# A third of the position bias made at the start of the kernel, its comparisons on GpSimd

## The chip, the cores and the metric

The kernel runs on one NeuronCore of one Trainium2 chip. The metric is the device time of one execution in microseconds (us), taken as the median of several runs. The engines are TensorE (PE in the profile; its weight loads stand apart as PEld), VectorE (DVE), ScalarE (ACT), GpSimd (POOL) and SyncE (SP), which here does nothing but issue transfers. Each engine works through its own queue in order; semaphores tie the queues together.

## The reference

A decoder trunk of two layers on 256 tokens of width 1024. Each layer is a half-step feed-forward network (FFN), an attention, and a second FFN half-step, each behind an RMS norm whose shift, scale and gate come from a conditioning vector `c`. The attention of the first layer adds a learned bias that depends on the bucket of the distance between two positions and on the head. Cut to what matters here:

```python
D_MODEL, SEQ, D_FF, MOBA_HEADS, REL_BUCKETS = 1024, 256, 2816, 16, 32

def swiglu(h, w_gate, w_up, w_down):
    return (jax.nn.silu(h @ w_gate) * (h @ w_up)) @ w_down
...
    c_act = jax.nn.silu(c)
    for layer in range(DEPTH):
        mods = c_act @ ada_w[layer] + ada_b[layer]
        sh1, sc1, g1, sh2, sc2, g2, sh3, sc3, g3 = jnp.split(mods, 9, axis=-1)
        h = modulate(rms_norm(x, norm_g[layer, 0]), sh1, sc1)
        x = x + 0.5 * g1[:, None, :] * swiglu(h, ffn_w_gate[layer, 0], ffn_w_up[layer, 0], ffn_w_down[layer, 0])
        ...
# inside the first layer's attention
        bias = bias_t[h5, t5_bucket(qp[:, None, :, None, None] - kpos)]
        s = jnp.einsum("bhqd,bhqnkd->bhqnk", qc, kg).astype(jnp.float32) * scale + bias.astype(jnp.float32)
        mask = (kidx <= qi[None, None, :, None, None]) & sv[None, None, :, :, None]
        s = jnp.where(mask, s, NEG)
```

## The kernel before, in words

All weights are float32 and are read once from HBM, 264 MB in all. A product of two float32 matrices is made on TensorE as three products of a rounded part ("hi") and the rest ("lo"): ScalarE makes hi from the raw tile (line 699 for the weights of most of the kernel), VectorE makes lo as raw minus hi (line 700), and the result is hi·hi + hi·lo + lo·hi. The conditioning vectors are not made on TensorE: VectorE multiplies tiles of `ada_w` with the broadcast of silu(`c`), called `c_b`, and sums (line 713, "a column dot" below).

**The start** is the function `first`. It makes the first 768 of the 2816 columns of gate and up of the first FFN while their weights and the first shift and scale come in, in eight chunks k = 0 to 7 of 128 rows of the input. Before chunk 0: silu(`c`) and its hi and lo (lines 1762 to 1764), eight small matmuls that broadcast it into PSUM (1768), two copies into `c_b` (1771), the sum of squares of the two halves of the tokens x0 and x1 (1789 on VectorE, 1786 on ScalarE), their root on GpSimd (`rstd`, line 889), two diagonal matrices of it (`diag`, 1793), and the scaled transposes of x (1803 for k = 0 and 1, 1808 after). Then for each chunk: two column dots (713) and one small scaling (717), `z` (1820), hi and lo of the input `h` (867, 868), hi and lo of the weights (`whi` 1831, `wlo` 1832), and 36 matmuls into six accumulators (1840 to 1842). TensorE multiplies zeros (1779, 1810) where it would have nothing to do.

**The bias** is the generator `bias_steps`. It is cut into 12 blocks: 4 groups c of 32 keys for each of three pairs of a query half t and a key half kb. For 8 comparison rows i of a group one comparison each, "query position at least key position plus bucket edge", gives a matrix of 0 and 1 in bf16 (`oh`): the even i on VectorE (line 1417, `is_ge`), the odd ones on ScalarE (1415, `Sign`, which gives -1 and 1 and so has its own table of halves). For kb = 0 it covers both query halves, 128x256. A block is then 24 matmuls (line 1396) of `oh` with three bf16 parts of the table of bucket steps (`tab`), a copy out of PSUM into `bt` (1403 on VectorE, which adds the causal mask where t equals kb, 1405 on ScalarE otherwise), and a store to `bias_d` in HBM (1406), from where the attention reads it back (1451). What comes before is `own`, `least`, `key`, `below`, `blk`, `rows` and the six parts of `tab`: small VectorE instructions (1365 to 1389), and 32 memsets of `low` on GpSimd (1359). The generator is stepped in the FFN after the start, among the matmuls of lines 1081 and 1087; `hold` keeps all of it behind a modelled time of 40 us (`HELD`).

**The order** of the work is not that of the code. The class `Order` takes all instructions with what they depend on, places them on the engines by a table of durations, and writes the order down for each engine; `ranked` gives an instruction a rank that puts it early, `hold` a time before which it isn't placed. It then tries disturbed orders, one for each seed of the list `TRIALS`, and keeps the best by its own table. The rank and the seeds so decide each queue, and the queue decides what waits behind what.

**The buffers** that the change touches: `ps_mm` has four PSUM banks (`mm_tile`), `ps_tr` four (`tr_tile`); `modp` has two SBUF tiles of 128x1024 called `gate`, first used for a gate vector at 144 us.

Of the kernel before, what the change touches and what calls it, by code (L numbers as in the profile page):

```python
# [31 lines left out]
B1 = 6  # L32
# [30 lines left out]
EARLY = 2  # L63
SIDE_TO = 6
# [129 lines left out]
def bcast_row(ap, n, parts=P):  # L194
# [21 lines left out]
TRIALS = (200001, 200002, 200017, 200027, 200038, 200039, 200043, 200053, 200064, 200109, 200195, 200238, 200274,  # L216
          200368, 200395, 200459, 200494, 200524, 200550, 200577, 200753, 200848, 200852, 200862, 200928, 201042,
          201579, 201676, 202214, 202513, 202702, 202901, 203186, 203712, 204111, 204899, 207186)
# [377 lines left out]
def trunk(ctx: ExitStack, tc: tile.TileContext, a: dict, out: bass.AP):  # L596
# [742 lines left out]
    groups = []  # L1339

    def bias_steps():
# [6 lines left out]
        with ExitStack() as st:  # L1348
            bp = st.enter_context(tc.tile_pool(name="bp", bufs=1))
            posi = bp.tile([P, S], I32, name="posi")  # L1350
            nc.sync.dma_start(posi, bcast_row(pos_f, S))
            btab = bp.tile([P, 3 * H + NT * NB], F32, name="btab")
            nc.sync.dma_start(btab, a["tab"])
            tab, prev, end = [btab[:, i * H:(i + 1) * H] for i in range(3)]
            keyi = btab[:, 3 * H:].bitcast(I32).rearrange("p (t b) -> p t b", t=NT)
            yield
# [3 lines left out]
            yield  # L1360
# [3 lines left out]
            posq = bp.tile([P, S], F32, name="posq")  # L1364
# [7 lines left out]
            yield  # L1372
# [3 lines left out]
            def parts():  # L1376
                blk = bp.tile([P, 4], F32, name="blk")
                V.tensor_reduce(blk, ident.rearrange("p (j b) -> p j b", b=NB), axis=AX.X, op=ALU.add)
                V.tensor_tensor(tab, prev, tab, op=ALU.subtract)
                for signs in range(2):  # L1380
                    rows = bp.tile([P, 4, H], F32, tag="rows", name=nm("rows"))
                    if signs:
                        V.tensor_tensor(tab, tab, end, op=ALU.subtract)
                    V.scalar_tensor_tensor(rows, blk[:, :, None].to_broadcast([P, 4, H]), 0.5 if signs else 1.0,
                                           tab[:, None, :].to_broadcast([P, 4, H]), op0=ALU.mult, op1=ALU.mult)
                    for i in range(3):
                        V.tensor_copy(pieces[signs][i], rows)
                        if i < 2:
                            V.tensor_tensor(rows, rows, pieces[signs][i], op=ALU.subtract)
            groups.append(parts)  # L1390

            def mms(kb, t, c, oh):
                pt = tr_tile()
# [499 lines left out]
```

## Time and profile before

| | |
|---|---|
| median of 3 runs | 974.61 us (974.39 to 976.02) |
| the profiled execution | 975.75 us, its span 974.0 us |
| TensorE, weight loads, VectorE, ScalarE, GpSimd busy | 99%, 85%, 89%, 64%, 7% |
| granted clock of TensorE | 1.00 |
| read from HBM, mean rate | 258.5 MB, 270 GB/s |

The span runs from the first to the last instruction of the profiled execution; its own time is 1.75 us more. In the timeline a row begins with the start in us from the span's start and the duration in us, then engine, line, operation, output and inputs, shape and count; what stands in square brackets is idle time of the engine before the row and what ended it. Rows of like instructions in a row are merged (x and a count). A matmul's duration covers its way through a pipelined array, so the distance between the starts of two neighbours, and not the duration, is what one costs.

### The profile page before, as it was taken

What the parts mean: (1) busy time and instruction counts of PE and PEld (TensorE: products, weight loads), DVE (VectorE), ACT (ScalarE), POOL (GpSimd) and SP (SyncE); (2) the same over time, 40 slices, a digit from 0 to 9 for tenths busy, and PEclk for the clock granted to TensorE, in tenths of its full rate; (3) what the DMA queues carried; (4) which work ended last, traced back from release to release, by engine and by line L of the source; (5) the groups of instructions that cost most, each with busy time, mean ns of one, the idle gap of its engine ahead of it and who ended that gap; (6) DMA issues with size and microseconds to landing.
All of it is one profiled execution on the core that took longest, in us unless ns stands there. A gap on an engine that the chain in (4) does not pass through costs nothing.

```text
span 974.0 us, 15262 instructions
## 1 busy us (share of the span) xinstructions
PE 962.7 (99%) x5516; PEld 823.7 (85%) x5516; DVE 871.2 (89%) x1587; ACT 618.6 (64%) x1158; POOL 70.0 (7%) x112
## 2 busy tenths in 40 slices
PE   8999999999999999999999999999999999999998
PEld 6988888888888788888888888888888888888887
DVE  7999899799999999999789999986899889768998
ACT  5697565378757965665367655553769886566561
POOL 1000000012230100000000000000143010000000
PEclk9999999999999999999999999999999999999999
DMA  9968789888886688888978798994533476544542
GB/s 368 409 226 298 293 315 360 319 306 332 285 319 225 236 310 344 324 341 312 362 299 320 289 344 339 353 351 172 171 110 116 150 278 254 192 173 175 198 180 81
DMA packets 54283, 263.73 MB, mean 271 GB/s; under 512 B 6304, under 2 KB 7104, under 8 KB 35904
## 3 DMA queue, kind: packets, MB, share of 16 engines
q1 hardware_dynamic: 51840, 255.93, 70.1%
q0 software_dynamic: 1888, 6.32, 2.1%
q8 instruction: 43, 0.70, 0.3%
q10 hardware_dynamic: 480, 0.51, 0.2%
q14 instruction: 32, 0.26, 0.1%
HBM read 258.52 MB, written 4.22 MB: 270 GB/s over the span
## 4 chain that ended last, share of the span: by engine, by line
PE 86%; DVE 5%; DMA 5%; issue 1%; ACT 1%; POOL 0%; SPq 0%; ACTq 0%; DVEq 0%
PE mm L1081 23%; PE mm L852 14%; PE mm L854 14%; PE mm L853 14%; PE mm L1087 12%; DMA raw<-in_first_dram 3%; DVE lo L700 2%; PE at L1294 1%; PE at L1237 1%; PE at L1274 1%; PE tr L902 1%; DMA raw<-in_w_dram 1%; PE mm L1634 1%; DMA bias_d<-bt 1%; PE tr L1670 1%
## 5 line engine op out<-in xcount | busy, mean ns | idle before, releaser
L699 ACT ACTIVATE hi<-raw 128x1024 fp32r<-128x1024 f32 (+1 forms) x308 | 312.5, 1035 | 148.4 <-PE mm L854 81.9
L700 DVE TENSOR_TENSOR lo<-raw,hi 128x1024 fp32r<-128x1024 f32 (+1 forms) x308 | 359.8, 1194 | 31.7 <-ACT hi L699 31.2
L1081 PE MATMUL mm<-h,hi 128*128 128x512 f32 x1120 | 263.5, 391 | 0.9 <-DVE g L1001 0.9
L1081 PEld LDWEIGHTS mm<-h,hi 128*128 128x128 f32 x1120 | 207.7, 188 | 42.7 <-DVE g L1001 1.3
L713 DVE CUSTOM_DVE_ANT_0 adaw<-adaw,c_b,cols 128x1024 f32<-128x1024 f32 x160 | 201.4, 1278 | 4.8 <-DMA adaw<-in_ada_dram 2.5
L1087 PEld LDWEIGHTS mm<-h,lo 128*128 128x128 f32 x1120 | 139.4, 192 | 2.7
L1087 PE MATMUL mm<-h,lo 128*128 128x256 f32 x1120 | 141.2, 283 | 0.0
L854 PE MATMUL mm<-hi,gl 128*128 128x512 f32 (+1 forms) x322 | 124.9, 388 | 0.0
L853 PE MATMUL mm<-lo,gh 128*128 128x512 f32 (+1 forms) x322 | 124.9, 388 | 0.0
L852 PE MATMUL mm<-hi,gh 128*128 128x512 f32 (+1 forms) x322 | 124.7, 389 | 0.0
L852 PE MATMUL mm<-hi,h 128*128 128x512 f32 (+1 forms) x240 | 94.2, 398 | 0.0
L853 PE MATMUL mm<-lo,h 128*128 128x512 f32 (+1 forms) x240 | 93.0, 391 | 0.0
L854 PE MATMUL mm<-hi,h 128*128 128x512 f32 (+1 forms) x240 | 91.8, 390 | 0.0
L854 PEld LDWEIGHTS mm<-hi,gl 128*128 128x128 f32 x322 | 60.5, 188 | 12.4
L853 PEld LDWEIGHTS mm<-lo,gh 128*128 128x128 f32 x322 | 60.5, 188 | 12.2
L852 PEld LDWEIGHTS mm<-hi,gh 128*128 128x128 f32 x322 | 60.5, 188 | 12.2 <-DVE u L1001 0.2
L1000 ACT ACTIVATE g<-mm 128x256 f32<-128x256 f32 x70 | 26.6, 380 | 57.2 <-PE mm L1087 57.0
L852 PEld LDWEIGHTS mm<-hi,h 128*128 128x128 f32 x240 | 45.1, 188 | 9.3 <-issue 1.3
L854 PEld LDWEIGHTS mm<-hi,h 128*128 128x128 f32 x240 | 45.1, 188 | 8.8 <-issue 0.2
L853 PEld LDWEIGHTS mm<-lo,h 128*128 128x128 f32 x240 | 45.0, 188 | 7.8
L1001 DVE TENSOR_TENSOR g<-mm,g 128x256 f32<-128x256 f32 x70 | 29.5, 421 | 20.4 <-ACT g L1000 19.2
L1331 POOL TENSOR_TENSOR hr<-hv,mhalf 128x4 f32<-128x4 f32 (+1 forms) x24 | 37.4, 1562 | 64.7 <-DVE hv L1330 59.5
(260 smaller groups left out, 1230.9 us busy)
## 6 DMA issues: line engine op xcount, KB each, us to landing
raw<-in_w_dram SPq DMA_DIRECT2D x143, 1024.0 KB, 5.5
adaw<-in_ada_dram SPq DMA_DIRECT2D x160, 512.0 KB, 6.0
raw<-in_w_dram SPq DMA_DIRECT2D x10, 512.0 KB, 4.8
raw<-in_first_dram SPq DMA_DIRECT2D x7, 512.0 KB, 9.0
bias_d<-bt SPq DMA_DIRECT2D x12, 256.0 KB, 4.4
gate<-gate_d POOLq DMA_DIRECT2D x6, 512.0 KB, 6.7
bg<-bias_d POOLq DMA_DIRECT2D x4, 768.0 KB, 5.9
raw<-in_first_dram SPq DMA_DIRECT2D x10, 256.0 KB, 8.9
```

The source lines that it names most:

```text
L699: nc.scalar.activation(hi, src, AF.Copy)
L700: nc.vector.tensor_tensor(lo, src, hi.bitcast(F32), op=ALU.subtract)
L713: nc.vector.tensor_tensor_reduce(wt, wt, c_b, 1.0, start, op0=ALU.mult, op1=ALU.add, accum_out=col)
L852: nc.tensor.matmul(ps, lh, rh, start=start, stop=False)
L853: nc.tensor.matmul(ps, lh, rl, start=False, stop=False)
L854: nc.tensor.matmul(ps, ll, rh, start=False, stop=stop)
L902: nc.tensor.transpose(kslice(pt, j), kslice(y, j), ident)
L1000: nc.scalar.activation(x, ps[:, S:], AF.Copy)
L1001: nc.vector.tensor_tensor(x, ps[:, :S], x, op=ALU.add)
L1081: nc.tensor.matmul(ps, wh, both, start=k == 0, stop=False)
L1087: nc.tensor.matmul(ps, wl, hh, start=False, stop=stop)
L1331: nc.gpsimd.tensor_tensor(r, v2, mhalf[:, :nh], op=ALU.pow)
```

## The change

Four of the 12 blocks, those of key half 0 with c = 0 and 1, are made in `first`, ahead of chunk 0. The positions, the table, `key`, the first three parts of `tab` and the comparisons come to the front. Of the 16 comparisons of 128x256, 14 are GpSimd's (`BY_POOL`: all i but 6) and 2 are VectorE's; all use `is_ge`. The mask is added by a matmul of the identity with the bf16 mask, not by VectorE. The four blocks accumulate in the four banks of `ps_mm`, are copied by ScalarE (`FORE_COPY`) into the two `gate` tiles, and are stored from there, not before a modelled time of 48 us (`FORE_OUT`). Four of the six accumulators of the first weights now take over those banks, two take `ps_tr`. The transfer of `cols` moves from ScalarE's queue to GpSimd's. After `first` the pool of the gate tiles `gh` and `gl` is opened anew. The seeds are others, so the order may differ anywhere.

On GpSimd the queue begins, after five constants, like this before; `ssq` is the sum of squares of a half of the tokens, `inv` a table for later, `low` the bucket edges:

```order
masks.py:197 MEMSET ident 128x128
masks.py:199 ISA
masks.py:199 AFFINE_SELECT ident<-ident 128x128
L674 MEMSET mask 128x256
L675 AFFINE_SELECT mask<-mask 128x256
L889 TENSOR_TENSOR rstd_215<-ssq_38_212,mhalf 128x1
L889 TENSOR_TENSOR rstd_222<-ssq_41_218,mhalf 128x1
L1531 MEMSET inv 128x1 x16
L1359 MEMSET low 128x1 x32
```

Now the same place reads, from the two casts of the identity and the mask on; `oh_180` are the comparisons of c = 0, `oh_181` those of c = 1:

```order
L1411 CAST mask_b<-mask 128x128
L1410 CAST ident_b<-ident 128x128
L1400 TENSOR_SCALAR oh_180<-posi,key 128x256 x5
L896 TENSOR_TENSOR rstd_418<-ssq_47_415,mhalf 128x1
L1400 TENSOR_SCALAR oh_181<-posi,key 128x256 x2
L896 TENSOR_TENSOR rstd_425<-ssq_50_421,mhalf 128x1
L1400 TENSOR_SCALAR oh_181<-posi,key 128x256 x2
L1400 TENSOR_SCALAR oh_180<-posi,key 128x256 x2
L1400 TENSOR_SCALAR oh_181<-posi,key 128x256 x3
L1568 MEMSET inv 128x1 x16
```

The root of the first half stands behind five comparisons, that of the second behind seven, and seven more follow; the transfer of `cols`, the 32 memsets and the two casts stand ahead of them all.

On TensorE the first matmuls of chunk 0 (line 1840, into the accumulators mm and tr) stand in the order before right behind the last scaled transpose:

```order
L1810 LDWEIGHTS zeros
L1810 MATMUL tr_190<-zeros 128x128
L1803 MATMUL tr_189<-diag_221,x_100 128x128
L1840 MATMUL mm_193<-h_106,whi_258 128x256
L1840 MATMUL mm_194<-h_106,whi_258 128x256
L1840 MATMUL mm_192<-h_106,whi_258 128x256
L1840 MATMUL tr_195<-h_106,whi_258 128x256
```

In the order now they stand behind the last of the 96 products of the four blocks (line 1405, into mm_282 to mm_284):

```order
L1405 MATMUL mm_284<-tab_161,oh_181 128x64
L1405 LDWEIGHTS oh_181
L1405 MATMUL mm_284<-tab_162,oh_181 128x64
L1851 LDWEIGHTS zeros
L1851 MATMUL tr_280<-zeros 128x128
...
L1881 MATMUL tr_403<-h_106,whi_461 128x256
L1882 MATMUL tr_403<-h_106,whi_461 128x256
L1881 MATMUL tr_404<-h_106,whi_461 128x256
L1849 MATMUL tr_279<-ident,y_455 128x128
```

All 96 products came ahead of chunk 0, so chunk 0 can't begin before the last comparison is done.

On VectorE the work between the lo part of silu(`c`) and the first column dot was one sum of squares (here "ISA", like the dots):

```order
L1764 TENSOR_TENSOR c_117<-c_115,c_116 32x256
L1789 ISA raw_144,ssq_38_212<-x_99 128x1024
L1789 ISA ssq_38_212 128x1
L713 ISA adaw_126,m_cols<-adaw_126,c_b,cols 128x1024
L713 ISA m_cols 128x1
```

It is now, from the same sum of squares on (its head, from `key` to the first part of `tab`, is left out here):

```order
L1830 ISA raw_234,ssq_47_415<-x_99 128x1024
L1830 ISA ssq_47_415 128x1
L1394 TENSOR_TENSOR rows_172<-rows_172,tab_160 128x64
L1392 CAST tab_161<-rows_172 128x64
L1394 TENSOR_TENSOR rows_172<-rows_172,tab_161 128x64
L1392 CAST tab_162<-rows_172 128x64
L1400 TENSOR_SCALAR oh_180<-posi,key 128x256
L1400 TENSOR_SCALAR oh_181<-posi,key 128x256
L720 ISA adaw_215,m_cols<-adaw_215,c_b,cols 128x1024
```

The rest of the table and two comparisons moved in between the sum of squares and the first column dot.

The diff, cut to its core:

```diff
+FORE = 2
+BY_POOL = (0, 1, 2, 3, 4, 5, 7)
+FORE_OUT = 48e3
+FORE_RANK = 6.5
+FORE_COPY = (lambda nc, o, i: nc.scalar.activation(o, i, AF.Copy), lambda nc, o, i: nc.scalar.activation(o, i, AF.Copy))
...
-TRIALS = (200001, 200002, 200017, ...
+TRIALS = (100002, 100006, 100008, ...
...
             if start:
                 start(units)
+                gq = st.enter_context(tc.tile_pool(name=nm("gp"), bufs=1))
...
-            bp = st.enter_context(tc.tile_pool(name="bp", bufs=1))
+            bp = st.enter_context(tc.tile_pool(name="bp", bufs=1, side="right"))
...
+            def onehot(kb, m, to, how):
+                if how == "sign":
+                    nc.scalar.activation(to, posq[:, kb * P:], AF.Sign, bias=below[:, kb, m:m + 1])
+                else:
+                    how.tensor_scalar(to, posq[:, kb * P:], key[:, kb, m:m + 1], None, op0=ALU.is_ge)
...
+            ident_b, mask_b = [bp.tile([P, P], BF16, name=n) for n in ("ident_b", "mask_b")]
+            nc.gpsimd.tensor_copy(ident_b, ident)
+            nc.gpsimd.tensor_copy(mask_b, mask[:, P:])
+            parts(0)
+            ohs = [bp.tile([P, 8, S], BF16, tag="oh", name=nm("oh"), bufs=2) for _ in range(FORE)]
+            for c, oh in enumerate(ohs):
+                for i in range(8):
+                    onehot(0, 8 * c + i, oh[:, i], nc.gpsimd if i in BY_POOL else V)
+
+            def fore(c, t, pt):
+                home = fore_home[c][:, t * 512:(t + 1) * 512]
+                if t == 0:
+                    ahead_of = mask_b[:, NB * c:NB * (c + 1)]
+                    nc.tensor.matmul(pt, ident_b, ahead_of[:, :, None].to_broadcast([P, NB, H]), start=True, stop=False)
+                products(0, t, ohs[c], pt, False, t > 0)
+                bt, pv = home.rearrange("p (h k) -> p h k", h=H), pt.rearrange("p (m h) -> p h m", h=H)
+                with ranked(FORE_RANK):
+                    FORE_COPY[t](nc, bt, pv)
+                hold(lambda: nc.sync.dma_start(bias_d[t, c], home), FORE_OUT)
...
             for kb in range(NT):
                 n = P * (NT - kb)
-                for c in range(4):
-                    oh = bp.tile([P, 8, n], BF16, tag="oh", name=nm("oh"), bufs=3)
+                for c in range(0 if kb else FORE, 4):
+                    oh = bp.tile([P, 8, n], BF16, tag="oh", name=nm("oh"), bufs=2)
...
         with ExitStack() as st:
+            next(side[0])
             fp = st.enter_context(tc.tile_pool(name="fp", bufs=1))
...
-                nc.scalar.dma_start(all_cols, a["cols"])
+                nc.gpsimd.dma_start(all_cols, a["cols"])
...
-            accs = [tr_tile() if f >= 4 else mm_tile() for f in range(B1)]
-            for f in range(B1):
-                for i in range(4 if 1 <= f < 4 else 1):
-                    nc.tensor.matmul(accs[f], zeros, zeros[:, None].to_broadcast([P, 4, P]), start=i == 0, stop=False)
+            fore = [mm_tile() for _ in fore_groups]
+            for ps in fore[:3]:
+                for i in range(4):
+                    nc.tensor.matmul(ps, zeros, zeros[:, None].to_broadcast([P, 4, P]), start=i == 0, stop=i == 3)
+            for ps, fn in zip(fore, fore_groups):
+                fn(ps)
+            accs = [tr_tile() if f < 2 else mm_tile() for f in range(B1)]
+            for ps in accs:
+                nc.tensor.matmul(ps, zeros, zeros[:, None].to_broadcast([P, 4, P]), start=True, stop=False)
```

More of the change, by code (lines that the diff above doesn't have):

```diff
@@ L1371, in bias_steps @@
             V.tensor_scalar(below, key, -1.0, 0.5, op0=ALU.mult, op1=ALU.add)
-            yield
-            pieces = [[bp.tile([P, 4, H], BF16, name=f"tab{i}{j}") for j in range(3)] for i in range(2)]
[L1376 to L1389, printed above, removed]
@@ L1390, in bias_steps, with parts @@
-            groups.append(parts)
+            pieces = [[bp.tile([P, 4, H], BF16, name=f"tab{i}{j}") for j in range(3)] for i in range(2)]
+            blk = bp.tile([P, 4], F32, name="blk")
+            V.tensor_reduce(blk, ident.rearrange("p (j b) -> p j b", b=NB), axis=AX.X, op=ALU.add)
+            def parts(signs):
+                rows = bp.tile([P, 4, H], F32, tag="rows", name=nm("rows"))
+                V.tensor_tensor(tab, tab if signs else prev, end if signs else tab, op=ALU.subtract)
+                V.scalar_tensor_tensor(rows, blk[:, :, None].to_broadcast([P, 4, H]), 0.5 if signs else 1.0,
+                                       tab[:, None, :].to_broadcast([P, 4, H]), op0=ALU.mult, op1=ALU.mult)
+                for i in range(3):
+                    V.tensor_copy(pieces[signs][i], rows)
+                    if i < 2:
+                        V.tensor_tensor(rows, rows, pieces[signs][i], op=ALU.subtract)
@@ new lines, in onehot, with products @@
+            def onehot(kb, m, to, how):
[3 more added lines that the diff above has]
+                    how.tensor_scalar(to, posq[:, kb * P:], key[:, kb, m:m + 1], None, op0=ALU.is_ge)
+            def products(kb, t, oh, pt, signs, first=True):
+                for i in range(8):
+                    for pi in range(3):
+                        nc.tensor.matmul(pt[:, i * 64:(i + 1) * 64], oh[:, i, (t - kb) * P:(t - kb + 1) * P],
+                                         pieces[i % 2 if signs else 0][pi], start=first and pi == 0,
+                                         stop=pi == 2 and (first or i == 7))
@@ L1392, in mms @@
+            fore_home = [modp.tile([P, D], F32, tag="gate", name=nm("fore")) for _ in range(FORE)]
+            for c in range(FORE):
+                for t in range(NT):
+                    fore_groups.append(lambda pt, c=c, t=t: fore(c, t, pt))
+            yield
+            parts(1)
             def mms(kb, t, c, oh):
                 pt = tr_tile()
-                for i in range(8):
-                    for pi in range(3):
-                        nc.tensor.matmul(pt[:, i * 64:(i + 1) * 64],
-                             oh[:, i, (t - kb) * P:(t - kb + 1) * P], pieces[i % 2][pi], start=pi == 0, stop=pi == 2)
+                products(kb, t, oh, pt, True)
```

23 lines of the change are left out of this document (9 added, 14 removed), and 4 rows, old and new, of the table TRIALS.

## The prediction

> **What bounds the kernel now.** I read the page's busy shares and its chain of waits first, then busy times of four stages (columns: PE, PEld, DVE, ACT, POOL busy in us, granted clock, DMA share, GB/s), then the timeline of the first stage.
>
> ```profile
> span 974.0 us, 15262 instructions
> PE 962.7 (99%) x5516; PEld 823.7 (85%) x5516; DVE 871.2 (89%) x1587; ACT 618.6 (64%) x1158; POOL 70.0 (7%) x112
> PE 86%; DVE 5%; DMA 5%; issue 1%; ACT 1%; POOL 0%; SPq 0%; ACTq 0%; DVEq 0%
> 0.00:12.18 12.18, 8.48 (x42) 4.70 (x42) 6.73 (x18) 7.97 (x17) 3.02 (x26) 1.00 0.86 332
> 12.18:30.00 17.82, 16.74 (x137) 16.33 (x138) 16.48 (x29) 9.54 (x17) 0.00 (x0) 1.00 1.03 405
> 30.00:50.30 20.30, 20.15 (x166) 19.48 (x165) 20.12 (x39) 14.55 (x25) 0.00 (x0) 1.00 1.03 410
> 50.30:116.00 65.70, 65.70 (x610) 57.55 (x609) 60.57 (x142) 50.08 (x104) 1.12 (x32) 1.00 0.73 261
> ```
>
> From 50 us on TensorE is the bound: a product taken off its queue there is worth its own length. From 12.18 to 50.3 us, the eight chunks, three things are close to full at once: transfers (share 1.03), VectorE (idle 1.34 + 0.18 = 1.5 us) and TensorE. Before 12.18 us TensorE has nothing to multiply but zeros, and GpSimd hardly works.
>
> ```profile
> 0.99 5.31 PE L1779 MATMUL mm<-zeros 128*128 128x512 bf16 x13 [0.99 <-DVE zeros L1724]
> 4.83 1.21 DVE L1789 CUSTOM_DVE_ANT_0 raw<-x 128x1024 f32<-128x1024 f32 x1
> 6.13 0.57 POOL L889 TENSOR_TENSOR rstd<-ssq,mhalf 128x1 f32<-128x1 f32 x1 [4.09 <-DVE ssq L1789]
> 8.24 0.69 ACT L1793 ACTIVATE diag<-ident,rstd 128x128 f32<-128x128 f32 x2
> 8.39 1.28 DVE L713 CUSTOM_DVE_ANT_0 adaw<-adaw,c_b,cols 128x1024 f32<-128x1024 f32 x1 [2.34 <-ACT c_b L1771]
> 9.23 1.32 ACT L1831 ACTIVATE whi<-raw 128x512 fp32r<-128x512 f32 x2 [0.30 <-DMA raw<-in_first_dram]
> 11.13 0.55 ACT L1820 ACTIVATE z<-tr,m_cols 128x256 f32<-128x256 f32 x1
> 12.16 0.43 DVE L868 TENSOR_TENSOR h<-z,h 128x256 fp32r<-128x256 f32 x1
> 12.18 0.62 PE L1840 MATMUL mm<-h,whi 128*128 128x256 f32 x3 [1.43 <-ACT h L867]
> 49.30 0.28 PE L1842 MATMUL tr<-h,wlo 128*128 128x256 f32 x1
> 50.25 0.28 PE L1842 MATMUL tr<-h,wlo 128*128 128x256 f32 x1
> ACT whi L1831 <- DMA raw<-in_first_dram: 12.6, 8, 2.7
> DVE adaw L713 <- DMA adaw<-in_ada_dram: 1.1, 1, 1.1
> ```
>
> The chunks start when `h` is there (12.18). The last two L1842 rows bracket eight starts: 0.95 / 8 = 0.119 us per matmul. 288 of them and 12 transposes at about the same make 35.7 us of the 38.2 between 12.18 and the end, so TensorE can start 2.5 us later and lose nothing. ScalarE waits 12.6 us for raw weights and has room; VectorE waits 1.1 for a transfer and has almost none.
>
> **What leaves the stage after 50 us.** Four of 12 blocks, 96 of 288 products.
>
> ```profile
> L1396 PE MATMUL tr<-tab,oh 128*128 128x64 bf16 x288 | 11.0, 194 | 0.0
> 70.21 0.84 PE L1396 MATMUL tr<-tab,oh 128*128 128x64 bf16 x23
> 71.21 0.87 PE L1396 MATMUL tr<-tab,oh 128*128 128x64 bf16 x24
> 50.53 7.30 PE mm L1081 x32
> L1417 DVE TENSOR_SCALAR oh<-posq,key 128x256 bf16<-128x256 f32 (+1 forms) x32 | 8.7, 311 | 0.0
> L1387 DVE CAST tab<-rows 128x64 bf16<-128x64 f32 x6 | 1.2, 193 | 0.0
> L1403 DVE TENSOR_TENSOR bt<-tr,mask 128x512 f32<-128x512 f32 x8 | 5.4, 681 | 0.9 <-PE tr L1396 0.9
> L1405 ACT ACTIVATE bt<-tr 128x512 f32<-128x512 f32 x4 | 2.4, 590 | 0.2 <-PE tr L1396 0.2
> 116.97 0.73 PE L1081 MATMUL mm<-h,hi 128*128 128x512 f32 x2 [0.86 <-DVE g L1001]
> ```
>
> From 70.21 to 71.21 lie one block's products and one matmul of 512 columns (7.30 / 32 = 0.23): 0.77 us a block with its switching, 3.1 us for four. VectorE loses there eight comparisons (0.31 each, 2.5), two masked copies (1.4) and some 17 small instructions (0.19 each by the casts, 3.2), 7 us of 60.57, so I take the 0.86 us stall at 117 as gone too. Gain: 4.0 us. Nothing before the end has a long hole, so it should arrive there. The four stores are the same bytes as before; put off to the time after 48 us, they meet a DMA share of 0.73, and the `gate` tiles aren't wanted until 144 us: no cost, unless a store were so late that the gate load waited for it.
>
> **What is added at the start.** The price of a GpSimd comparison of 128x256 stands in no row. The nearest:
>
> ```profile
> 1.01 0.29 POOL masks.py:199 TENSOR_SCALAR_AFFINE_SELECT ident<-ident 128x128 f32<-128x128 f32 x1
> 1.26 0.31 POOL L674 MEMSET mask<- 128x256 f32 x1
> 1.64 0.40 POOL L675 TENSOR_SCALAR_AFFINE_SELECT mask<-mask 128x256 f32<-128x256 f32 x1
> 50.65 1.12 POOL L1359 MEMSET low<- 128x1 f32 x32 [42.19 <-PE tr L1842]
> 138.10 0.71 POOL L753 DMA_DIRECT2D gate_d<-cols  x1 [86.33 <-DVE cols L1564]
> 328.56 1.28 DVE L713 CUSTOM_DVE_ANT_0 adaw<-adaw,c_b,cols 128x1024 f32<-128x1024 f32 x1
> 328.72 1.53 POOL L889 TENSOR_TENSOR rstd<-ssq,mhalf 128x1 f32<-128x1 f32 x1 [8.15 <-DVE ssq L882]
> 706.35 0.55 DVE L868 TENSOR_TENSOR qlT<-tr,qlT 128x384 fp32r<-128x384 f32 x1
> 706.58 0.55 POOL L1594 TENSOR_TENSOR rstd<-var,mhalf 128x1 f32<-128x1 f32 x1 [6.19 <-DVE var L1592]
> cols<-in_cols_dram ACTq DMA_DIRECT2D x1, 147.0 KB, 5.0
> ```
>
> A select reads and writes the same size: 0.40, and neighbours overlap by 0.04 (1.01 + 0.29 against 1.26): 0.36. Below it stands the memset's 0.31, which reads nothing; above, the root's 0.57, of one element. I take 0.36 to 0.40, nearest in kind, and keep 0.31 and 0.6 as ends.
>
> A second price is the wait for VectorE. The same root takes 0.55 to 0.57 us when VectorE is idle or reads one operand from PSUM (706.35), and 1.53 beside a dot whose operands are both in SBUF: the dot ends at 329.84, the root 0.41 later. So a GpSimd instruction that reads can't get in while such a VectorE instruction runs. That VectorE is held in turn by a reading GpSimd no row shows; I bound it by 0 and the comparison's length and take 0.3.
>
> The Trainium skill (the page "SBUF — State Buffer", section "Who interferes with whom") says that a VectorE instruction with two SBUF inputs contends with a GpSimd instruction that reads SBUF, and that the second to come blocks fully. The roots agree with the first half (1.53 against 0.55); by the second VectorE would be held for the whole 0.40, and the loss on VectorE below would be 0.3 us more.
>
> Now the queue. `key` needs `low` and the identity: GpSimd's transfer of `cols` (0.71), 32 memsets (1.12), the identity's and the mask's memsets (0.31 at most each) and one select put the identity at 3.4 us; seven small VectorE instructions (0.19 each, 1.4) and the lo part of silu(`c`) follow: 5.2 us. The positions stand first on SyncE's queue, so x and the weights come one issue later; with the table they are 0.19 MB, 0.46 us at 405 GB/s. That is hidden as long as VectorE runs later than the transfers, and costs 0.5 if not. `cols` lands about 6 us (5.0 after its issue), its first reader comes at 9.3.
>
> From 5.2 to 9.3 VectorE has a sum of squares (1.21, two SBUF inputs), eight small instructions and two comparisons, then the dots without a break (0.9 us later than before). GpSimd does in that time about five comparisons, the first root and the sixth. If the seventh reads before the first dot, the second root is done at 11.2; if not, it and the seventh wait for one dot each, and it is 12.3. Behind this root hang `diag` (0.4), then on ScalarE's queue the weights' two hi parts and a small one (1.5), `z`, and `h`: 14.1 or 15.2 on VectorE against 12.16. With three or four comparisons holding VectorE for 0.3, less its 1.5 us of idle, VectorE's end of the stage moves by 1.3 or 2.7. The other seven comparisons run while VectorE waits for `z`, and later between its `wlo`: done at 15.0 or 16.6, chunk 0 at 15.3 or 16.9, that is 3.1 or 4.7 late. Add the zeroing of four accumulators, 0.23 each, now among the chunks (0.9), less 2.5 of room: TensorE ends the stage 1.5 or 3.1 later. The four copies of 0.59 on ScalarE stand ahead of chunk 1's weights and wait for the last products: the same delay, taken from its 12.6 us of room. The mask's two matmuls and the 96 products lie in idle time, all but the last six (0.2, counted). I take the middle: 2.3 us lost.
>
> Sum: 2.3 - 4.0 = -1.7. The profiled execution, 975.75 (span 974.0 and 1.75 around it), would become 974.05; it stands 1.14 above the median shown, so the median becomes 972.9.
>
> **Rivals.** *The cover holds.* Comparisons at 0.31 put both roots ahead of the dots; chunk 0 starts by 14.5, TensorE loses 0.7 and VectorE nothing: 971.3. For it: before, GpSimd did nothing between the select at 1.64 and the first root at 6.13. Against: seven comparisons, two roots and the sum of squares are 4.5 us from 5.2 on, already at the edge.
>
> The Trainium skill ("GPSIMD Engine Reference", "4.1 Engine selection") calls one-input elementwise work on GpSimd roughly line-rate; 256 elements at its 1.2 GHz are an estimate of 0.21 us and a dispatch. By it this rival would be likelier; no run here shows it.
>
> *The comparisons are dear, and the kernel gets slower.* At 0.6 each the 14 take 2.8 us more than at 0.40, all ahead of chunk 0: 5.9 lost, 976.5; at 0.8, 979.3. It decides from chunk 0 starting at 17.8 on (12.18 + 4.0 + 2.5 - 0.9), where the loss passes 4.0.
>
> *TensorE starts slow.* The first 13 matmuls of 512 columns take 5.31 / 13 = 0.41 each, later 0.23 is normal. If three products per comparison let it fall back, the first 5 us of the chunks run at half pace: 2.5 more lost, 975.4.
>
> The Trainium skill ("TensorE: Matmul & The Clock Gate", "Part 1: The HAM clock gate") has the clock halved after an idle window of about 3.4 us; the start agrees (0.41), the granted clock in the rows (1.00) doesn't show it.
>
> *Only the order.* The new seeds win or lose some 2 us anywhere: 971 or 975 whatever the start does.
>
> **Numbers.** 0.2% (about 1.95 us) is the least that a measurement can tell. Forecast, 971.5 to 974.5: 0.42, of it 0.18 faster and 0.24 within. Cover holds: 0.20, faster. Dear comparisons: 0.24, of it 0.18 slower. Slow TensorE: 0.07, 0.05 within. Order: 0.07, mostly faster or slower alike, 0.03 each. Faster 0.41, same 0.36, slower 0.23. The range leaves out the best of the cover and the dearest comparisons: 970.4 to 977.2.
>
> **What would show it.** GpSimd's rows of the comparisons: under 0.4 when VectorE is idle, over 1.2 beside dots. The first matmul of chunk 0 between 15 and 17 us; the first L1081 equivalent at 52 to 53.5 instead of 50.37; by 120 us the place in the program 1 to 3 us earlier than before. Wrong would be: comparisons of 0.6 and more, VectorE rows stretched beside them, matmuls of chunk 0 at 0.24, or a difference that arises after 120 us.

## The result and the profile after

The changed kernel takes 987.74 us (median of 4 runs, 986.84 to 989.02) against 974.93 of the kernel before (median of 4): ratio 1.0131, 95% interval 1.0113 to 1.0148. It is 12.8 us slower; the forecast was 972.9 (970.4 to 977.2). The profiled execution took 988.44.

The page of the kernel after, its span, its busy shares and the shares of its chain of waits:

```profile
span 986.7 us, 15280 instructions
PE 970.5 (98%) x5521; PEld 828.0 (84%) x5521; DVE 870.6 (88%) x1579; ACT 616.5 (62%) x1152; POOL 86.9 (9%) x129
PE 94%; POOL 2%; DMA 1%; ACT 1%; DVE 1%; issue 0%; ACTq 0%; SPq 0%; DVEq 0%
```

GpSimd is 17 us busier than before, and the chain now goes through it for 2% of the span. The same four stages of the kernel after (PE, PEld, DVE, ACT, POOL busy, granted clock, DMA share, GB/s):

```profile
0.00:12.18 12.18, 8.12 (x22) 3.60 (x22) 8.26 (x29) 4.43 (x8) 8.53 (x47) 1.00 0.80 288
12.18:30.00 17.82, 11.20 (x131) 9.65 (x131) 8.99 (x15) 8.75 (x18) 13.60 (x29) 0.74 1.03 406
30.00:50.30 20.30, 20.30 (x167) 20.02 (x167) 16.84 (x31) 10.79 (x19) 0.00 (x0) 0.98 0.66 246
50.30:116.00 65.70, 65.70 (x575) 59.46 (x573) 64.79 (x136) 49.81 (x99) 0.00 (x0) 1.00 0.88 312
```

From 12.18 to 30 us TensorE, VectorE and ScalarE work half to two thirds of the time (VectorE 8.99 of 17.82, before 16.48), and TensorE's clock is granted at 0.74 in the mean (0.50 from 13.8 to 17.1 and from 24.1 to 30.8 us, 1.00 between and after). What GpSimd does there, from its timeline in the kernel after:

```profile
7.26 6.79 POOL L1400 TENSOR_SCALAR oh<-posi,key 128x256 bf16<-128x256 f32 x5 [2.52 <-DVE btab L1388]
14.03 0.57 POOL L896 TENSOR_TENSOR rstd<-ssq,mhalf 128x1 f32<-128x1 f32 x1
14.60 1.82 POOL L1400 TENSOR_SCALAR oh<-posi,key 128x256 bf16<-128x256 f32 x2
16.39 0.56 POOL L896 TENSOR_TENSOR rstd<-ssq,mhalf 128x1 f32<-128x1 f32 x1
16.95 8.36 POOL L1400 TENSOR_SCALAR oh<-posi,key 128x256 bf16<-128x256 f32 x7
```

It works without a break from 7.26 to 25.31 us on 14 comparisons and two roots, and the chain of waits that ends in chunk 0's matmuls runs through it all that time (comparisons are 55% of that chain in the first 31 us). Who waits for it, in the timelines of VectorE, ScalarE and TensorE of the kernel after:

```profile
6.90 0.25 DVE L1377 TENSOR_SCALAR key<-btab,least 128x64 f32<-128x64 int32 x1 [1.15 <-DMA btab<-in_tab_dram]
22.14 1.48 DVE L720 CUSTOM_DVE_ANT_0 adaw<-adaw,c_b,cols 128x1024 f32<-128x1024 f32 x1
16.99 0.40 ACT L1834 ACTIVATE diag<-ident,rstd 128x128 f32<-128x128 f32 x1 [1.96 <-POOL rstd L896]
21.64 0.70 PE L1405 MATMUL mm<-tab,oh 128*128 128x64 bf16 x18 [2.61 <-POOL oh L1400]
26.59 0.56 PE L1881 MATMUL tr<-h,whi 128*128 128x256 f32 x1
...
28.23 0.41 PE L1881 MATMUL tr<-h,whi 128*128 128x256 f32 x1
28.44 0.41 PE L1882 MATMUL tr<-h,whi 128*128 128x256 f32 x1
```

`key` waits for the table until 6.90; the second `diag` stands at 16.99 (before at 8.5); chunk 0 begins at 26.59 (before 12.18), and its matmuls start 0.21 us apart (28.23, 28.44; before 0.12). Where the lost time goes can be followed by three stations on TensorE: the first matmul of the FFN after the start, the first gate product at 150 us, and the last FFN matmul. The answer for one line gives the first and last start of a group (shortest, median, longest in ns stand ahead). The kernel after:

```profile
L1089 PE MATMUL mm<-h,hi x1120: 387/389/483, 65.7 to 921.8; 128*128 128x512 f32 x187
L861 PE MATMUL mm<-hi,gl x322: 283/389/483, 160.9 to 980.9; 128*128 128x512 f32 x159, 128*128 128x256 f32 x2
```

The kernel before in a second profile (its span is 972.7; the experiment called "The kernel before once more" says why it is the better measure):

```profile
L1081 PE MATMUL mm<-h,hi x1120: 387/389/481, 50.5 to 907.8; 128*128 128x512 f32 x187
L854 PE MATMUL mm<-hi,gl x322: 283/389/481, 149.7 to 967.0; 128*128 128x512 f32 x159, 128*128 128x256 f32 x2
```

So the kernel after is 15.2 us late at the first station, 11.2 at the second and 13.9 at the third: 15.2 lost at the start, 4.0 given back by 150 us, 2.7 lost again between about 690 and 790 us. The spans differ by 14.0 (986.7 - 972.7). The medians differ by 12.8, because the profiled execution of the kernel after lies 0.7 above its median and the second one of before (974.51) 0.4 below.

This table holds the runs; lateness is against the second profile of before, in us, from the same rows of each run, each of a single profiled execution. That of the run with all comparisons on VectorE (e2) took 991.58, 4.3 above its median, so part of its lateness belongs to that execution. The expectations of the runs up to e11 were written before that profile was there and count against the first, which runs 1.2 us later from 117 us on.

| run | median, ratio to before (95%) | chunk 0's first matmul into ps_tr, into ps_mm | late at 50 | late at 150 | late at the end |
|---|---|---|---|---|---|
| after | 987.74, 1.0131 (1.0113 to 1.0148) | 26.6, 30.6 | 15.2 | 11.2 | 13.9 |
| e1_narrow | 979.93, 1.0056 (1.0041 to 1.0072) | 18.8, 21.0 | 5.5 | 1.5 | 4.1 |
| e2_vector | 987.28, 1.0139 (1.0117 to 1.0162) | 16.3, 29.3 | 13.6 | 9.6 | 17.0 |
| e3_told | 987.53, 1.0132 (1.0116 to 1.0149) | 15.9, 28.6 | 12.5 | 9.0 | 13.1 |
| e4_probe (before) | 976.51, one run | 12.9, 12.4 | -0.1 | 2.1 | 2.0 |
| e5_vector_early | 981.69, 1.0069 (1.0054 to 1.0084) | 18.1, 18.5 | 6.0 | 1.8 | 6.3 |
| e6_split | 978.70, 1.0038 (1.0025 to 1.0051) | 15.8, 16.1 | 4.4 | 0.1 | 3.9 |
| e7_one | 988.95, 1.0140 (1.0124 to 1.0155) | 21.3, 22.9 | 8.8 | 6.7 | 14.4 |
| e8_seeds (before) | 980.03, 1.0049 (1.0033 to 1.0064) | 13.1, 11.6 | -0.1 | -0.1 | 6.2 |
| e9_split_seeds | 976.07, 1.0016 (1.0007 to 1.0025) | 15.5, 16.9 | 3.5 | -0.1 | 1.5 |
| e10_before_seeds | 974.39, 0.9998 (0.9989 to 1.0007) | 12.9, 12.5 | -0.8 | -0.1 | -0.2 |
| e11_warm | 998.43, 1.0243 (1.0228 to 1.0259) | 37.2, 37.5 | 23.4 | 21.0 | 24.3 |
| e12_before_again (before) | 974.51, one run | 12.8, 12.3 | 0 | 0 | 0 |
| e13_x_between | 977.13, 1.0029 (1.0018 to 1.0040) | 17.0, 18.5 | 5.0 | 1.5 | 3.8 |
| e14_x_first | 977.46, 1.0032 (1.0020 to 1.0044) | 18.0, 18.2 | 5.9 | 2.7 | 2.8 |

### The profile page after: what moved, and what is told of

Read it like the earlier page. It is cut to its first block, busy times and chain, and to the rows that moved or that the text cites. A ratio compares the mean times of both kernels' runs of the same rounds, so it can differ in the third digit from the quotient of the medians.

```text
span 986.7 us, 15280 instructions
## 1 busy us (share of the span) xinstructions
PE 970.5 (98%) x5521; PEld 828.0 (84%) x5521; DVE 870.6 (88%) x1579; ACT 616.5 (62%) x1152; POOL 86.9 (9%) x129
## 4 chain that ended last, share of the span: by engine, by line
PE 94%; POOL 2%; DMA 1%; ACT 1%; DVE 1%; issue 0%; ACTq 0%; SPq 0%; DVEq 0%
PE mm L1089 26%; PE mm L859 14%; PE mm L861 14%; PE mm L860 14%; PE mm L1095 14%; POOL oh L1400 2%; PE at L1302 1%; PE at L1245 1%; PE at L1282 1%; PE tr L909 1%; PE mm L1881 1%; PE mm L1882 1%; PE mm L1883 1%; PE tr L1707 1%; PE mm L1671 1%; DMA wkv<-in_w_dram 1%
## 5 line engine op out<-in xcount | busy, mean ns | idle before, releaser
L861 PEld LDWEIGHTS mm<-hi,gl 128*128 128x128 f32 x322 | 60.5, 188 | 12.4
L860 PEld LDWEIGHTS mm<-lo,gh 128*128 128x128 f32 x322 | 60.5, 188 | 12.3
```

Of the source, the lines that this page charges most:

```text
L860: nc.tensor.matmul(ps, lh, rl, start=False, stop=False)
L861: nc.tensor.matmul(ps, ll, rh, start=False, stop=stop)
```

## The experiments

**The comparisons made short, the order kept.** The order of every engine is that of the changed kernel, since the planner is told the old price; only the work of each GpSimd comparison shrinks (a quarter of the columns is compared, so the early blocks leave out the rest).

```diff
+            if kind == "InstTensorScalarPtr" and n == 64:
+                d = 140.0 + 1.22 * 256
...
+                elif how is nc.gpsimd:
+                    how.tensor_scalar(to[:, :64], posq[:, :64], key[:, kb, m:m + 1], None, op0=ALU.is_ge)
...
+                        if not signs and i in BY_POOL:
+                            w = oh[:, i, t * 32:t * 32 + 1].to_broadcast([P, P])
```

> The changed kernel with the same order on every engine; only the 14 comparisons of GpSimd cover 64 of their 256 query positions, and the products read one column of them for all (so the four early blocks are not the reference's). Theory A, the price of a GpSimd comparison times its elements sets the start: a comparison falls from 0.91 to about 0.3 us alone (0.91 x 64 / 256 = 0.23 and something fixed), the run of 14 comparisons and two roots, 18.05 us long, to 6 to 8, the first matmul of chunk 0 from 26.59 to 15 to 17 us, the time to 976 to 979. Rival B, what is late is the rest (the key at 6.90, all 96 products ahead of chunk 0 in TensorE's queue): chunk 0 stays above 20 us and the time above 983. Rival C, the price is fixed per instruction and not per element: comparisons stay near 0.9 us, time 987 to 988.

The comparisons of the kernel after, and those of this run with its two stations (shortest, median, longest in ns); the row that ends in idle time gives the busy us of the group and the mean ns:

```profile
L1400 POOL TENSOR_SCALAR oh<-posi,key x14: 912/1247/1697, 7.3 to 24.4; 128x256 bf16<-128x256 f32 x14
L1400 POOL TENSOR_SCALAR oh<-posi,key 128x256 bf16<-128x256 f32 x14 | 17.0, 1225 | 2.5 <-DVE btab L1388 2.5
```

```profile
L1402 POOL TENSOR_SCALAR oh<-posi,key x14: 435/442/1524, 7.5 to 17.7; 128x64 bf16<-128x64 f32 x14
L1402 POOL TENSOR_SCALAR oh<-posi,key 128x64 bf16<-128x64 f32 x14 | 8.6, 644 | 2.8 <-DVE btab L1390 2.8
L1091 PE MATMUL mm<-h,hi x1120: 387/389/483, 56.0 to 912.0; 128*128 128x512 f32 x187
L863 PE MATMUL mm<-hi,gl x322: 283/389/485, 151.2 to 971.1; 128*128 128x512 f32 x159, 128*128 128x256 f32 x2
```

By theory A it should be 976 to 979; 979.93 is just beyond it, with chunk 0 at 18.8 instead of 15 to 17: a short comparison costs 0.44 alone and not 0.3, and 0.64 in the mean, for three of them still take 1.08 to 1.52 beside VectorE's work. Rivals B (chunk 0 above 20 us) and C (0.9 each) fall. Of the 15.2 us at the start, 9.7 go with the length of the comparisons alone, and 5.5 stay. The 4.0 given back by 150 us is the same, and the 2.6 lost later is nearly the 2.7, so neither hangs on GpSimd.

**What a comparison costs by itself.** Instructions that nobody reads, on GpSimd in the kernel before.

```diff
+                for n in (256, 128, 64, 16):
+                    G.tensor_scalar(trial[0][:, :n], posq[:, :n], key[:, 0, 0:1], None, op0=ALU.is_ge)
+                G.tensor_scalar(trial[1], posq, key[:, 0, 0:1], None, op0=ALU.is_ge)
+                G.tensor_scalar(trial[0], posq, 0.5, None, op0=ALU.is_ge)
+                G.tensor_copy(trial[2], posq)
...
```

> The kernel before with 30 instructions on GpSimd added between 50 and 120 us whose results nobody reads: comparisons of 256, 128, 64 and 16 columns, with f32 output, with bf16 input, with a constant instead of the per-partition scalar, casts, copies and memsets of 128x256. Theory A: price by element, so 0.9 / 0.5 / 0.3 / 0.1 us for 256 / 128 / 64 / 16 when VectorE isn't in a two-operand SBUF instruction, 0.5 more beside one. Rival C: fixed, all near 0.9. If the constant form costs 0.3 like the casts (0.28 for 128x128 before), it is the per-partition scalar that makes it dear; if a cast of 128x256 takes 0.5 and the constant form 0.9, it is the comparison itself.

The groups by line, in that order: comparisons of four widths, cast from f32 to bf16, comparison with f32 output, copy, comparison with a constant:

```profile
L1376 POOL TENSOR_SCALAR trial<-posq,key x12: 322/602/1965, 57.7 to 77.9; 128x256 bf16<-128x256 f32 x3, 128x128 bf16<-128x128 f32 x3, 128x64 bf16<-128x64 f32 x3, 128x16 bf16<-128x16 f32 x3
L1379 POOL CAST trial<-posq x3: 387/440/1409, 58.8 to 72.7; 128x256 bf16<-128x256 f32 x3
L1377 POOL TENSOR_SCALAR trial<-posq,key x3: 915/916/1192, 59.7 to 65.2; 128x256 f32<-128x256 f32 x3
L1381 POOL COPY trial<-posq x3: 390/392/531, 61.4 to 67.7; 128x256 f32<-128x256 f32 x3
L1378 POOL TENSOR_SCALAR trial<-posq x3: 847/868/988, 62.9 to 78.3; 128x256 bf16<-128x256 f32 x3
```

Shortest of each: 0.32 us for 16 columns (first row), 0.44 for 64 (the run above), 0.91 for 256, that is about 0.28 fixed and 2.5 ns a column. A cast or a copy of the same 256 columns takes 0.39; a constant instead of the per-partition value saves 0.07, f32 output nothing. So the per-partition value is not what makes it dear, and the select from which the prediction took its price (0.40) costs what a copy does. Whether it is the comparison or any `tensor_scalar` on GpSimd isn't shown: no run timed another arithmetic operation of it. The copy also stands near what the Trainium skill ("GPSIMD Engine Reference", "4.1 Engine selection") says of one-input work, roughly line-rate (an estimate of 0.21 us from its 1.2 GHz, without dispatch); for the comparison the trace does not agree.

**Nobody on GpSimd.** `BY_POOL = ()` gives all 16 to VectorE.

> The changed kernel with all 16 comparisons on VectorE (0.31 us each by its own rows), none on GpSimd; the order is worked out anew. Theory A, GpSimd's price and its hold on VectorE: 16 x 0.31 = 5.0 us come onto VectorE in the first 50 us, half of them in its gaps; roots are not queued behind anything; chunk 0 at 13.5 to 16 us; 974 to 978 in all. Rival B, early blocks cost that much by themselves (late key, 96 products and their copies out of the accumulators' banks): above 982 whoever compares.

Theory A failed here: 987.28, as by rival B, though not for the reason that it gave, as the run with the comparisons together shows below. VectorE's and TensorE's timelines:

```profile
25.24 1.13 DVE L1400 TENSOR_SCALAR oh<-posi,key 128x256 bf16<-128x256 f32 x4
26.80 1.13 DVE L1400 TENSOR_SCALAR oh<-posi,key 128x256 bf16<-128x256 f32 x4
27.55 1.49 PE L1405 MATMUL mm<-tab,oh 128*128 128x64 bf16 x24
29.24 0.58 PE L1820 MATMUL mm<-zeros 128*128 128x512 bf16 x1 [0.20 <-ACT fore L68]
```

The new order strews the comparisons and puts eight of them behind the third pair of dots, though each needs only 0.27. Until a block is multiplied and copied it holds its bank of `ps_mm`, and the first copy starts only at 28.59: chunk 0 starts at 16.3 into the two accumulators in `ps_tr`, but the first matmul into a `ps_mm` accumulator is at 29.3. So it isn't enough to take the comparisons off GpSimd; it also counts when the last one is done.

**The planner told the price.** One line more in its table, `d = 140.0 + 4.6 * n` (ns, for n columns) for a comparison on GpSimd.

> The changed kernel; only the planner's table is told that a GpSimd comparison of 128x256 takes 1.32 us instead of 0.45, so the order is another: roots ahead of most comparisons, and chunk 0's matmuls into the two ps_tr accumulators ahead of most of the 96 products. Theory A, the price itself: GpSimd still needs some 17 us for 14 comparisons from 7.3 us on, the four ps_mm accumulators come free only at about 25 us, so the four share columns wait and the wait moves rather than goes: chunk 0 begins at 14 to 16 us, the stage ends 4 to 10 us late, 978 to 984. Rival D, the order was the fault and a planner that knows the price hides it: under 976.

GpSimd's timeline and TensorE's first matmuls of the chunks:

```profile
13.86 14.52 POOL L1402 TENSOR_SCALAR oh<-posi,key 128x256 bf16<-128x256 f32 x11
L1883 PE MATMUL mm<-h,whi x64: 277/281/775, 28.6 to 62.6; 128*128 128x256 f32 x64
```

Both roots are now done by 13.86 and chunk 0 starts at 15.9, but eleven comparisons follow, and `ps_mm` comes free at 28.6. The wait moved, as theory A has it; the loss at 50 us is 12.5, more than the 10 it allowed, 4.1 are lost after 150, and 987.53 lies above its 978 to 984. Rival D falls.

**The comparisons early and together.** As the run with all on VectorE, with a rank that puts them ahead of the dots.

```diff
+            with ranked(1.4):
                 parts(0)
...
+                    with ranked(1.5):
+                        onehot(0, 8 * c + i, oh[:, i], V)
```

> As the run with all 16 comparisons on VectorE, but ranked so that they stand together ahead of the first column dot; there they were strewn to 27.9 us, and the first matmul into a ps_mm accumulator came at 29.26, 1.3 us after the last of them. Theory A2, four of the six accumulators of the first weights are the banks of the early blocks, so the chunks can't run before the last comparison is made, on whatever engine: the last comparison ends at about 15 us, the dots move behind them to 15 to 17.5, chunk 0 starts at 17 to 19 us and is not held up by banks; the place in the program at 56 us is 4 to 7 us late instead of 13.7, by 150 us 1 us early to 2 us late. The end then hangs on the order in the stage from 690 to 760 us, which cost 2.6 to 7.4 in the three orders seen: 975 to 983. Rival, not the banks but the extra work as such (VectorE, products, late key): it stays at 13 late at 56 us and near 987.

VectorE's row of the comparisons, and the first matmul of chunk 0:

```profile
10.05 4.32 DVE L1400 TENSOR_SCALAR oh<-posi,key 128x256 bf16<-128x256 f32 x16
18.14 0.51 PE L1883 MATMUL tr<-h,whi 128*128 128x256 f32 x2 [0.23 <-ACT h L874]
```

The same work on the same engine, done at 14.4 instead of 27.9: the first station falls from 13.6 to 6.0 late. Theory A2 holds; the rival falls.

**One group instead of two.** `FORE = 1`.

> The changed kernel with one group of 32 keys made early instead of two (FORE = 1): two blocks, 8 comparisons, 7 of them on GpSimd, two ps_mm banks. Theory A, price of GpSimd's comparisons: 7 x (0.91 to 1.43) and two roots take GpSimd from 7.3 to about 17 us; chunk 0 at about 18 us, 6 late, two accumulators later still or at once; 5 to 7 late at 56 us, 3 given back by 150 us (half of 5.3): 976 to 982 with the order cost. Rival, the loss hangs on the first comparison only (late key, the moved transfers): nearly as slow as with two groups, 985.

GpSimd and VectorE:

```profile
7.51 7.55 POOL L1400 TENSOR_SCALAR oh<-posi,key 128x256 bf16<-128x256 f32 x6 [3.37 <-DVE key L1377]
15.03 0.57 POOL L896 TENSOR_TENSOR rstd<-ssq,mhalf 128x1 f32<-128x1 f32 x1
18.39 0.69 DVE L1873 TENSOR_TENSOR wlo<-raw,whi 128x512 fp32r<-128x512 f32 x1 [4.94 <-ACT whi L1872]
```

Both expectations missed the time: half the blocks cost as much in all, 988.95. The rival had that form, but the start is not as late as with two groups (8.8 against 15.2), as theory A has it, if by more than its 5 to 7. Here the banks don't matter (`ps_mm` from 22.9). The first root, whose input was ready at 9.4, stands behind six comparisons until 15.03, and with it `diag`, ScalarE's weights and `z`; VectorE stands idle for 4.94. Two blocks give back 2.1 by 150 us, half of the 4.0 of four; the rest of the time is lost late (7.7 after 150).

**Half on ScalarE.** Odd rows as `Sign`, the table's second parts early, the table right behind the positions on SyncE's queue.

```diff
-                nc.scalar.dma_start(btab, a["tab"])
+                nc.sync.dma_start(btab, a["tab"])
...
+                    with ranked(1.5):
+                        onehot(0, 8 * c + i, oh[:, i], "sign" if i % 2 else V)
```

> Half of the 16 comparisons on VectorE (0.27 us apart), half on ScalarE as Sign (about 0.45 each, before ScalarE has weights to copy), ranked ahead of the dots; the second three parts of the table made early too; the table's transfer behind the positions on SyncE's queue instead of ScalarE's. Theory A2: key at about 5.5 us instead of 6.9, VectorE has 8 comparisons (2.2 us) and some 14 small instructions ahead of the dots, these start at 12 to 13, chunk 0 at 15.5 to 17; 3 to 5 us late at 56 us, 2 early to level at 150; with an order cost of 2 to 5 after 690 us, 974 to 979. If the early blocks were a loss by themselves: above 983.

978.70, as expected: 4.4 late at 50, level at 150, then 3.8 lost.

**The order alone, and a longer search.** First the kernel before with nothing but the changed kernel's `TRIALS`:

> The kernel before with only the list of seeds of the changed kernel. Theory, the 2.6 us that the changed kernel loses between 690 and 760 us are its seeds' order in that stage: 2 to 5 us slower than before, all of it arising there. Rival, they come from what the early blocks moved: within 1 us of before.

```profile
L1083 PE MATMUL mm<-h,hi x1120: 387/389/483, 50.4 to 914.1; 128*128 128x512 f32 x187
690.00:700.00 10.00, 7.57 (x37) 6.10 (x36) 9.53 (x25) 7.47 (x17) 0.55 (x1) 0.94 0.76 215
PE mm L1636 <- DMA wkv<-in_w_dram: 1.8, 1, 1.8
```

Nothing at 50 or 150 us, 6.2 at the end: the list of seeds by itself costs the kernel before 5.4 us (980.03 against 974.6), all after 150 us, so the theory holds, by a little more than its 5. Part of that loss goes with a low clock. Near 700 us TensorE waits 1.8 us for a transfer (`wkv`; 1.0 in before), and its granted clock is 0.94 and then 0.89 in the two stretches of 10 us from 690 to 710, which is up to 1.7 us of TensorE's time; the runs with all on VectorE and with one group wait 2.0 and 2.2 there, at 0.82 and 0.83 from 700 to 710. The kernel after waits 1.1 and stays at 1.00, so its 2.7 aren't of that kind. Then the split with a list from a longer search by the planner's table (and ranks 1.45 for parts and comparisons, 4.5 for the copies), beside the kernel before with as long a search:

> The split of the comparisons over VectorE and ScalarE (which was 1.06 us ahead of before at 150 us and 2.74 behind at the end), with a list of seeds from a longer search by the planner's own table, and the table's parts and the comparisons at one rank. Theory O, the order of the stage from 690 to 790 us is a loss apart from the early blocks and hangs on the seeds alone: the start stays 4 to 5 us late at 50 us and 0.5 to 1.5 ahead at 150, the later loss falls from 3.8 to between 0 and 2; 973 to 976. Rival P, early blocks cause the later loss (their buffers, stores or tiles): 3 to 4 us lost after 300 us again, 977 to 979.

> Control: the kernel before, its own seeds followed by as long a search for more; the planner's table finds 0.4 us. Theory O: the same start, and in the stage from 690 to 790 us another order by chance, between 1 us faster and 3 slower: 973.5 to 977.5. If it is faster than before by as much as the split with searched seeds, then the split's gain is the seeds'.

Theory O holds in kind: the split's late loss fell from 3.8 to 1.6, to 976.07; the search gave before nothing (0.9998). This is the best version with early blocks, and it does not beat before (1.0016).

**TensorE kept at work.** Five matmuls of zeros ahead of the products of each comparison.

```diff
+                    for _ in range(0 if first else 5):
+                        nc.tensor.matmul(pt, ident_b, warm[:, None].to_broadcast([P, 16, 32]), start=False, stop=False)
```

> The changed kernel with five more matmuls of zeros (512 columns) ahead of the products of each comparison for the first half of the queries, 80 in all, so that TensorE does not stand still while it waits for GpSimd. Theory C, the clock: the granted clock between 12 and 30 us is 0.95 or more instead of 0.74, chunk 0's matmuls start 0.12 us apart at once instead of 0.22, and the chunks end 2 to 3 us less behind chunk 0's first matmul than they did (changed kernel: first 14.4 late, last 14.6 late, though there is 2.5 of room). Rival, the clock costs nothing because transfers or VectorE set the chunks anyhow: last chunk matmul as late as before to within 1 us. The time follows with the order's chance of 3 us: 984 to 989.

The stage from 12.18 to 30 us and the first station:

```profile
12.18:30.00 17.82, 14.84 (x116) 7.52 (x115) 5.71 (x8) 6.32 (x12) 12.13 (x28) 1.00 1.03 406
L1089 PE MATMUL mm<-h,hi x1120: 387/389/500, 73.9 to 932.1; 128*128 128x512 f32 x187
```

As a kernel it failed (998.43, far over 984 to 989): the zeros stood ahead of the broadcast of `c_b` and delayed the dots. But the clock is 1.00 instead of 0.74, and from chunk 0's first matmul to the first station it takes 36.7 us (73.9 - 37.2) where the changed kernel takes 39.1 (65.7 - 26.6). 2.4 us are what the low clock costs by this at most: the weights were all there by then, and VectorE had dots done ahead (from 28.6 on), which helps this run too. The kernel after gives the same size by itself: at 0.50 from chunk 0's start at 26.6 to 30.8 us, TensorE loses up to 2.1.

**The kernel before once more.**

> The kernel before, unchanged, profiled a second time. The stall of TensorE at 117 us (a wait for VectorE, 0.86 us in the first profile) is missing in the three profiles of kernels whose work there is that of before (the one with probes on GpSimd, the two with other seeds). Theory S, it belongs to one execution and not to the kernel: it is missing here too, the span is 972.6 to 972.9 instead of 974.0. Then the gain that the prediction took for its going was never there. Rival, it belongs to the order of before and other seeds or probes removed it: 0.8 to 1.2 us of waiting at 117 us again, span near 974.

Its span, and TensorE's timeline at 117 us:

```profile
span 972.7 us, 15262 instructions
115.92 2.91 PE L1081 MATMUL mm<-h,hi 128*128 128x512 f32 x12
```

No stall: the row runs through where the first profile had [0.86 <-DVE g L1001]. Theory S holds: that wait was one execution's.

**What is left of the late start.** The split with the tokens ahead of the bias's transfers: one half (ranks 0.4 and 0.3, as below), or both (1.4 and 1.3). Each has a list of seeds of its own, so the late loss can't be compared.

```diff
-            with ranked(-0.01):
+            with ranked(0.4):
                 nc.sync.dma_start(posi, bcast_row(pos_f, S))
-            with ranked(-0.005):
+            with ranked(0.3):
                 nc.sync.dma_start(btab, a["tab"])
```

> The split, with SyncE's queue in another order: first half of the tokens, table, positions, second half (before: positions and table first, and the tokens landed some 6 us after their issue, at about 7.5 us, against 4.1 and about 5 in the kernel before; VectorE's sum of squares began at 7.14 instead of 4.83). Theory X, what is left of the late start (3.5 us at 50 us) is the tokens' transfer behind the bias's: the sum of squares begins at about 5, the first dot at 9.5 to 10.5 instead of 11.5, chunk 0 at 13.5 to 14.5 instead of 15.5; 1.5 to 2.5 us late at 50 us, 1.5 to 2.5 ahead at 150; with 0 to 3 lost in the order after 690 us, 971.5 to 976. Rival V, it is VectorE's extra work (8 comparisons, 14 small instructions, 4.5 us): the dots stay at 11 or later whenever the tokens come, 974.5 to 978.

> The same with both halves of the tokens ahead of table and positions. Theory X: sum of squares at 4.8 as before, key at 6 to 6.5, comparisons to 9.5, first dot at 9.5 to 10.5; 1.5 to 2.5 us late at 50 us, 971.5 to 976 by the order's chance. Rival V as in the run beside it.

VectorE of the first, sum of squares and first dot; then, of the second, the positions:

```profile
4.94 1.21 DVE L1828 CUSTOM_DVE_ANT_0 raw<-x 128x1024 f32<-128x1024 f32 x1
11.13 1.28 DVE L716 CUSTOM_DVE_ANT_0 adaw<-adaw,c_b,cols 128x1024 f32<-128x1024 f32 x1
```

```profile
9.10 0.68 DVE L1372 CAST posi<-posi 128x256 f32<-128x256 int32 x1 [2.30 <-DMA posi<-in_positions_dram]
```

Theory X falls and rival V holds (977.13): the tokens come in time, and the dots don't. From 6.17 to 11.13 VectorE has 5.0 us of comparisons and small instructions, where the kernel before had 2.3 us of idle time (6.04 to 8.39). With the positions behind the tokens, VectorE waits for them instead.

## Why the prediction was wrong

**The step that failed is the price of a GpSimd comparison**, a term of the sum under the heading of what is added at the start: taken as 0.36 to 0.40 with 0.6 as the upper end, it is 0.91 alone and 1.22 in the mean beside VectorE's work (17.0 us busy for 14). With that the start lost 15.2 us where the sum had 2.3, and with the comparisons made short, at the same order, 9.7 of the 15.2 went. The rival of dear comparisons had the mechanism: 3.1 lost at 0.40 and 14 us more for each us of price, so 976.5 at 0.6 and 979.3 at 0.8. At the mean of 1.22 its line gives 14.6 lost (measured 15.2) and 985.2, at the short comparisons' mean of 0.64 it gives 6.5 (measured 5.5); its point of decision (chunk 0 at 17.8) was passed by 8.8. The range was cut off at an end that came from instructions of another kind. That the line fits to about 1 us is in part luck, since other terms at the start were off too, as the next paragraphs say.

**Two-sided waiting** was right for GpSimd (comparisons up to 1.70 beside VectorE's two-operand work), too high for VectorE: of its four dots beside comparisons one is not held (1.27) and three are held by 0.14 to 0.21 (1.41 to 1.48), not 0.3. Two of them, from VectorE's timeline of the kernel after:

```profile
10.58 1.27 DVE L720 CUSTOM_DVE_ANT_0 adaw<-adaw,c_b,cols 128x1024 f32<-128x1024 f32 x1
20.80 1.41 DVE L720 CUSTOM_DVE_ANT_0 adaw<-adaw,c_b,cols 128x1024 f32<-128x1024 f32 x1
```

The full block that the prediction read in the Trainium skill ("SBUF — State Buffer", "Who interferes with whom") is spelled out there for VectorE's two-port modes; of two SBUF inputs the section says that they contend, under a general rule of an exclusive lock. The trace agrees that they contend, and it shows no dot held for a whole comparison (0.21 at most).

**The queue at the start** was right in form: roots behind comparisons, then `diag`, weights, `z`, `h`; the last comparison decides when chunk 0 can begin. The prediction saw TensorE's in-order queue as the reason; the runs with other orders show a second one that it did not name, the banks: chunk 0 may start, but `ps_mm` is held. In the kernel after itself two of the four banks were copied by 23.5 us, and there TensorE's queue kept chunk 0 back until 26.6. `key` at 5.2 was 1.7 early, since the table landed 5.6 us after its issue, and the first dot began at 10.58, 2.2 later than before, where the sum had 0.9. "One issue later and 0.46 us, hidden" was wrong as to size: the tokens landed 6.3 us after their issue instead of 4.1. It didn't matter next to VectorE's 5.0 us of added work, which even the best version could not hide: 3.5 late at 50 us. The room of 2.5 us on TensorE didn't help: from chunk 0 to the first station the kernel after takes 39.1 us, before 50.5 - 12.3 = 38.2, and 36.7 with the clock kept up. The low clock is up to 2.1 to 2.4 us of it, where the rival "TensorE starts slow" said 2.5; what the zeroing of banks takes isn't shown apart.

**The gain** came out at 4.0 us, as summed, but by luck, from other parts: four blocks give back 3.2 to 4.3 in most runs that have them (2.4 in the run with the matmuls of zeros), about 1.0 each instead of 0.77, and the 0.86 us stall was never the kernel's. The prediction took one execution's wait for a property.

**"Only the order"** held as a mechanism beside the rest, not instead of it: 2.7 us lost after 150 us, more than its 2.

All four marks that the prediction named as showing it wrong are in the trace: comparisons over 0.6, VectorE rows stretched (three of the four dots), chunk 0's first matmuls 0.21 us apart, a difference that arises after 120 us. The lateness of 13.9 is 15.2 - 4.0 + 2.7. Not settled: which placement in the stage from 690 to 790 us costs the 2.7, and how the 5.5 us that stay at the start with short comparisons divide between the waits for VectorE, VectorE's added work and the clock; no run took them apart.

## What to carry to other kernels

Price an operation on an engine from the same operation there, not from a neighbour of the same size; where no row has it, let the upper end of the range reach well over twice the nearest price, or time it first. Before filling an idle engine, look at what stands behind the new work in its queue and which buffers that work holds until its last instruction. Profile the kernel before twice, before a single stall is entered as a gain; and when an order is searched anew, run the old kernel with the new order as a control.

## What the runs showed of the hardware

A GpSimd comparison costs about 0.28 us and 2.5 ns a column, while its copy of 256 columns takes 0.39 and VectorE's comparison follows the next after 0.27 (16 in 4.32). A root of one element on GpSimd took 2.78 us in the run with all comparisons on VectorE, where two dots followed each other without a gap:

```profile
11.37 2.78 POOL L896 TENSOR_TENSOR rstd<-ssq,mhalf 128x1 f32<-128x1 f32 x1 [0.84 <-ACT ssq L1828]
```

Bursts of products between waits of 2 to 4 us went with a granted clock of TensorE of 0.74 over 18 us (0.50 in parts of it); with 80 matmuls of zeros in the waits it stayed at 1.00.
